# A hybrid GDN/RWKV decoder step: all weight rests computed on VectorE instead of partly on GpSimd

## The chip, the cores and the metric

The kernel runs on one core of a Trainium2 chip. The metric is the device time of one execution in microseconds (us), as the median of several executions. The profile used below is one further execution, seen through the hardware profiler. Engine names are those of the profile: PE is TensorE, PEld its weight loads, DVE is VectorE, ACT is ScalarE, POOL is GpSimd and SP is SyncE.

## The reference

The reference is one inference step of a two-layer decoder over 512 prompt tokens behind 16 meta tokens, and over 8 samples of 4 tokens. Model width is 1024. Layer 0 mixes tokens by a gated delta rule (GDN), layer 1 by RWKV-7, and each is followed by a channel mixer with a causal convolution (FFN). Cut to what matters here:

```
proj = h @ w_in                              # GDN: queries, keys, values, gate z: 4096 columns
qkv  = silu(causal_conv4(proj[:, :3072]))    # 24 feature tiles of 128
... per chunk: M = I + strict(kb k^T * decay); solve M [u w] = rhs     # triangular inverse
o    = recurrence over the chunks;  y = (norm(o) * silu(z)) @ w_out

k = xk @ wk;  r = xr @ wr;  v = xv @ wv      # RWKV: 8 feature tiles each
... per chunk a triangular inverse again, then the recurrence
x = x + (gate * ...) @ wo
x = x + (silu(conv3(h @ w_gate)) * (h @ w_upper)) @ w_down    # FFN, after each mixer
```

All of it is float32. The outputs are the tokens of the last layer and the states of both mixers and both convolutions.

## The kernel before, in words

**Products in parts.** All 560 token columns (32 of samples, 16 meta, 512 of the prompt) lie in the free dimension, and features lie on partitions, 8 tiles of 128. TensorE multiplies in float32r, which keeps fewer bits than float32, so each operand is split in two: a leading part `hi` and the rest `lo` = operand minus `hi`. A dense product is then `hi*xh + hi*xl + lo*xh` (`dense_g`, L98; its matmuls have line L113). One output tile of 128 features takes 8 k tiles x 3 products x 2 column halves = 48 matmuls. It goes to one of two PSUM tiles called `pd`.

**How a weight is prepared.** `load_piece` (L62) loads 128x1024 floats into `raw` (a DMA from ACT's queue, L67), copies them to `hi` on ACT (L68), and computes the rest on an engine that the caller names:

```
lo_eng.tensor_tensor(lo[:R, :kt, :M], raw[:R, :kt, :M], hi[:R, :kt, :M].bitcast(F32), op=ALU.subtract)   # L69
```

There are two buffers each of `raw`, `hi` and `lo`, and `fetch` (L92) keeps one weight ahead of the one in use. So the `hi` for weight n+2 can be written once PE has finished weight n, and its `lo` follows.

**The list of weights.** `plan` (L84) announces the weights of every dense product in the order of use, each with its engine for the rest; without one it is VectorE. `plan_gdn` (L397) and `plan_rwkv` (L958) name GpSimd for 30 of the 32 tiles of GDN's input weight (all but the first two), for the 24 tiles of RWKV's key, receptance and value weights and for one tile of its gate: 55 in all. The FFN weights (`w_up`, `w_down`), `gdn_out`, `w_o` and the thin ones are VectorE's already.

**What sets the order.** A class `Weave` (L326) emits dense pieces and small dependent steps ("chains") in turn, by a clock of its own. After that the tile framework lays out each engine's instructions with a timeline model of its own (`schedule_with_timeline_sim=True`). Each engine then runs its list strictly in order. An instruction that waits holds everything behind it on its engine.

**GDN's input** (25 to 318 us of the profile). The feature tiles come in the order keys, queries, values, z. Each of the first 24 goes through the convolution: DVE scales it out of PSUM into `gp` (L545, L547), ACT and POOL make two of its four taps (L556 to L558), DVE adds the other two (L560), ACT applies SiLU. Transposes on PE (L580, L731) then make token-major copies. For the decay masks DVE makes 32 tiles `L` (L517) that PE multiplies (L518). After the last keys, DVE inverts 32x32 triangular blocks row by row (`tri_inverse`, L382: products L392, sums L394); row i works on i x i elements. The blocks are then joined on PE by `merges` (L680: transposes L687 on DVE, matmuls L693 to L716, copies on ACT). The z tiles need one DVE instruction each (L745). The recurrence begins with PE's L852.

**RWKV** (865 to 1500 us). After low-rank products come the 8 key, 8 receptance and 8 value tiles. Beside them stand: the decays (`decays`, L1203: a scan L1206, L1215 and L1221 on DVE, exponentials on ACT, products on POOL), the mixing of neighbouring tokens (`produce`, L1132: L1134 and half of L1137 on DVE, the other half of L1137 on POOL), evacuation of each tile by DVE (L1246 and L1248 for keys, L1164 for receptances), the products of the chunks (L1312 on PE, L1319 on DVE, L1322 on POOL) and the triangular inverses on DVE (`tri_inplace`, L978: products L990, sums L992). Then the recurrence starts, a chain of small steps through PE, ACT and DVE (L1563 to L1604).

Of the kernel before, what the change touches and what calls it, by code (L numbers as in the profile page):

```python
# [22 lines left out]
KD = 8  # L23
# [49 lines left out]
def load_stack(E, src, R, lo, tag):  # L73
    """copies of a thin matrix below each other: the leading parts, but on rows lo the rests"""
    nc = E.nc
    raw = E.wp.tile([P, KD, P], F32, tag="raw", name="raw", bufs=2)
    hi = E.wp.tile([P, KD, P], F32R, tag=tag, name=tag)
    nc.scalar.dma_start(out=raw[:R], in_=src)
    nc.scalar.activation(hi[:R], raw[:R], AF.Copy)
    nc.vector.tensor_tensor(hi[lo], raw[lo], hi[lo].bitcast(F32), op=ALU.subtract)  # L80
    return hi


def plan(E, src, kts, M=P, eng=None, R=P):  # L84
    """announces the weights of a dense product, in the order of use"""
    k = 0
    for kt in kts:
        E.plan.append((src[:, k:k + kt, :], kt, M, eng or E.nc.vector, R))
        k += kt
# [8 lines left out]
def dense_g(E, kts, xs, split, M=P, hook=None, room=None):  # L98
    """xs: (xh, xl) per k tile; the announced weights in turn; yields after each k tile and
    returns a psum tile [128, 2, 512]"""  # L100
    nc = E.nc
    ps = (room or E.pd).tile([P, 2, 512], F32, tag="pd", name="pd")
    halves = [(0, 0, split), (1, split, T)]
    K = sum(kts)
    k = 0
    for kt in kts:
        fetch(E)
        hi, lo = E.ready.pop(0)
        for kk in range(kt):
            xh, xl = xs[k]  # L110
            for w, x in ((hi, xh), (hi, xl), (lo, xh)):
                for b, c0, c1 in halves:
                    nc.tensor.matmul(ps[:M, b, :c1 - c0], lhsT=w[:, kk, :M], rhs=x[:, c0:c1],  # L113
                                     start=(k == 0 and w is hi and x is xh),
                                     stop=(k == K - 1 and w is lo))
            if hook is not None:
                hook(k)
            k += 1
            yield 0.715
    return ps  # L120


def dense_halves(E, kts, xs, split):
    """dense, but all of the first tokens' products before the last tokens'"""
    nc = E.nc
    ps = E.pd.tile([P, 2, 512], F32, tag="pd", name="pd")
    w = []
    for kt in kts:
        fetch(E)
        hi, lo = E.ready.pop(0)  # L130
        w += [(hi[:, k, :], lo[:, k, :]) for k in range(kt)]
    for b, c0, c1 in ((0, 0, split), (1, split, T)):
        for k, ((hi, lo), (xh, xl)) in enumerate(zip(w, xs)):
            for i, (a, x) in enumerate(((hi, xh), (hi, xl), (lo, xh))):
                nc.tensor.matmul(ps[:, b, :c1 - c0], lhsT=a, rhs=x[:, c0:c1], start=(k == i == 0), stop=(k == len(xs) - 1 and i == 2))  # L135
    return ps
# [20 lines left out]
def big(E, dtype, name, ring):  # L157
    """room for 8 feature tiles, in one of two rings of two"""
    return E.xp.tile([P, KD, T], dtype, tag=f"big{ring}", name=name, bufs=2)


def big_pair(E, name, rings):
    """room for the two float32r parts of 8 feature tiles"""
    return [big(E, F32R, name, r) for r in rings]
# [6 lines left out]
def split_x(E, x, g, xh, xl):  # L171
    """hi/lo parts of x * g (g: per-partition column)"""
# [9 lines left out]
class Norm:  # L182
    """sum of squares over the feature tiles, then the per-token scale on all partitions"""
# [21 lines left out]
    def scale(self, bank):  # L205
        """1 / rms of each token, on all partitions (in the place of the sums); bank: gives psum banks"""
# [19 lines left out]
def first_input(E):  # L226
    """the inputs split, and their squares"""
# [23 lines left out]
def ffn(E, layer, xs, norm, ring, x_dram, sink):  # L251
    """xs: split inputs, not yet scaled; ring: room for the hidden tiles; sink(m, x_new)"""
# [58 lines left out]
def rsqrt(E, tp, out, x, shape, tag, rows=None):  # L311
    """out = x ** -0.5 on the vector engine: exponent seed, then three Newton steps"""
# [13 lines left out]
class Weave:  # L326
    """Order of the tensor engine's work. Slots: dense products, generators that yield the time of
    the piece just emitted; each has a gate. Chains: generators of small dependent steps that yield
    (tensor time, delay before the next step, psum banks); a chain's step goes first when its delay
    has passed by the clock of emitted work, dense pieces fill the time between."""  # L330
# [51 lines left out]
def tri_inverse(E, U, L, tmp, n, R, w=None):  # L382
    """L [n, R, R] strictly upper parts, U [n, R, w] columns of the identity (all of them if w is None):
    U becomes those columns of the unit upper inverse of I + L, row by row from the last"""
# [12 lines left out]
def plan_gdn(E):  # L397
    g = E.nc.gpsimd
    plan(E, E.I["w_ab"], [KD], 32)
    for m in (*range(8, 16), *range(8), *range(16, 32)):  # L400
        plan(E, E.I["w_in"][m], [KD], eng=None if m in (8, 9) else g)
    for m in range(KD):
        plan(E, E.I["gdn_out"][m], [KD])
# [15 lines left out]
def gdn(E, xp, norm, x_dram, sink):  # L419
# [4 lines left out]
    with st:  # L424
# [150 lines left out]
        def token_major(X, h, i):  # L575
            """a head's keys or queries by token, and their squared norms"""
# [10 lines left out]
        def masked(X, h, i):  # L587
            """products of a head's keys with X, times decay and weight"""
# [177 lines left out]
        # the first chunk's keys; the samples' parts as three stacks: leading, leading, rest  # L766
# [100 lines left out]
        def finish(c, n, o, rows, tok):  # L867
            """gated norm of a chunk's outputs, feature-major, in the place of its keys"""
# [89 lines left out]
def plan_rwkv(E):  # L958
# [5 lines left out]
    for n in ("w_k", "w_r", "w_v"):  # L964
        for m in range(KD):
            plan(E, I[n][m], [KD], eng=g)
    plan(E, I["w_g2a"], [KD], eng=g)
# [10 lines left out]
def tri_inplace(E, X, tmp, n, R):  # L978
    """X [n, R, R], strictly upper triangular L: becomes the inverse of I + L, row by row from the last"""
# [16 lines left out]
# the first products of the low-rank parts act on each token (0) and on the token before (1):  # L996
# (weights, [(columns, mix, token)])
# [4 lines left out]
def first_lora(E, name, parts):  # L1002
    """W with W (1 - mix) or W mix in its place"""
# [14 lines left out]
def rwkv(E, xp, norm, x_dram, sink):  # L1018
    """xp: split inputs, not yet scaled. The heads go through the recurrence in two halves (G): the dense
    products fill the tensor engine's time between the steps"""  # L1020
    nc, I, O = E.nc, E.I, E.O
    st = ExitStack()
    with st:
# [4 lines left out]
        # by chunk of 64 tokens (the first: samples, meta tokens, padding): [r | keys], [k | removal keys]  # L1028
# [34 lines left out]
        # its two parts, by the column that they take  # L1063
# [33 lines left out]
        # the token before: the states in the place of the samples' last tokens, the first in that of the last  # L1097
# [5 lines left out]
        def before(t, ps, tag, n):  # L1103
            """adds what comes of the token before"""
# [5 lines left out]
        # the leading parts twice below each other, for the two parts of the weights  # L1110
# [44 lines left out]
        def pieces(ps, t):  # L1155
            """chunk 0 and the other chunks: of a product split at 304, of a chunked tile"""
# [95 lines left out]
        def sums(m, sq):  # L1252
            """squared key norms, token-major on partitions 64..127"""
# [50 lines left out]
        def products(G, c):  # L1304
            """masked products of the keys' side with the queries' side of a chunk"""
            o, n = col64(c)
            # the two heads of a pair lie on different rows: each has its own bank
# [30 lines left out]
        def early(G):  # L1338
            """what the inverses need, ahead of the other products"""
# [49 lines left out]
        def merge(G, q):  # L1389
            """the blocks off the diagonal of the inverses of two chunks"""  # L1390
# [19 lines left out]
        def ktokens(G):  # L1410
            """[keys | removal keys] of a chunk, token-major, put by in DRAM; but for the first chunk with the
            decay to the chunk's end"""
# [109 lines left out]
        def rec(G):  # L1522
# [19 lines left out]
            # meta tokens  # L1542
# [28 lines left out]
            for c in range(1, 9):  # L1571
# [6 lines left out]
                # the last head with its queries too: what closes the group has to cover all rows  # L1578
# [40 lines left out]
        def outnorm(G, Yt, r, o, n, t, room, lock):  # L1619
            """group norm, gain, bonus and gate of n tokens, on rows r; t, room: storage"""  # L1620
# [174 lines left out]
def fm(v, w=1):  # L1795
    """[n*128] or [n*128, w] -> [128, n*w]"""
# [10 lines left out]
def prep(a):  # L1807
# [46 lines left out]
    # [8, 3, 3072] -> [24, 128, 8, 3]  # L1854
    d["gdn_state"] = np.ascontiguousarray(a["state_gdn_conv"][0].transpose(2, 0, 1).reshape(24, P, 8, 3))
    # [b, h, k, v] -> [h, k, b, v]
# [3 lines left out]
    # [2, 8, 2, 2816] -> [2, 128, 22, 8*2]  # L1860
# [29 lines left out]
    # [8, 1024] -> [128, 8 (tile), 8 (b)]  # L1890
    d["rwkv_shift"] = np.ascontiguousarray(a["state_rwkv_shift"][0].T.reshape(KD, P, 8).transpose(1, 0, 2))
    # [b, h, v, k] -> [pair, (h, k), b, v]
# [8 lines left out]
def body(nc, tc, I, O):  # L1901
    with ExitStack() as st:
# [27 lines left out]
        def then(make, ring, gain, dram):  # L1930
            """sink into storage that is taken when the first tile comes"""
# [51 lines left out]
```

## Time and profile before

| what | value |
|---|---|
| median of 3 executions | 1941.8 us (1935.6 to 1948.63) |
| profiled execution, its span | 1937.2 us |
| PE busy in it | 1812.7 us (94%) |
| DVE busy | 1166.1 us (60%) |
| ACT busy | 670.3 us (35%) |
| POOL busy | 693.9 us (36%) |
| `lo` on DVE (L69) | 163 instructions, 189.2 us |
| `lo` on POOL (L69) | 55 instructions, 138.4 us |
| mean TensorE clock granted | 0.953 of full speed |

The profiled execution has no time beside its span; the span is 4.6 us under the median and inside the range of the three. The two FFN stages (465 to 865 and 1500 to 1937 us) keep PE busy nearly throughout; the rest of the table's PE idle time lies in the two mixers. A row of the windows view gives a stretch's length and, for each engine, its busy time and number of instructions in it. A row of the waits view gives who waited for whom, the total in us, how often, and the longest. A row of the timeline gives start, duration, engine, line, operation and tiles.

### The profile page before, as it was taken

The page shows a single profiled execution, that of the slowest core. Times are in us where ns is not written, and L with a number is a line of the kernel's source. Part 1 is how long each engine was busy: PE and PEld are TensorE (multiplying, and loading weights), DVE is VectorE, ACT ScalarE, POOL GpSimd, SP SyncE. Part 2 cuts the span into 40 slices and gives each one's busy share as a digit, 9 for nine tenths or more (in the row PEclk, how much of TensorE's full clock was granted, in tenths as well). Part 3 has the DMA queues.
Part 4 walks back from the last instruction along what each step waited for, and adds up shares of the span by engine and source line. Part 5 has one row for each costly group of instructions (what it writes and reads, how often), then busy time and mean ns, then how long its engine had stood idle before and what let it go on. Part 6 is the DMA issues. An engine that isn't in the chain of part 4 may idle for free.

```text
span 1937.2 us, 36248 instructions
## 1 busy us (share of the span) xinstructions
PE 1812.7 (94%) x14673; PEld 1730.0 (89%) x14673; DVE 1166.1 (60%) x2090; ACT 670.3 (35%) x1250; POOL 693.9 (36%) x823
## 2 busy tenths in 40 slices
PE   7999899989999999998889989799998999999996
PEld 6888889789999999998688879688787999999996
DVE  6788952775555553335679898865565555554222
ACT  4775344442222222221872123113124222222221
POOL 4663732711222220113576464444444122221011
PEclk9999999999999999998888999797998999999998
DMA  4232223334222223343112224233237222222331
GB/s 129 76 88 83 66 76 125 142 101 141 77 88 88 88 82 101 118 143 93 61 54 51 85 85 137 87 101 77 84 92 234 95 81 83 88 88 89 99 106 67
DMA packets 125704, 186.44 MB, mean 96 GB/s; under 512 B 60785, under 2 KB 73073, under 8 KB 125537
## 3 DMA queue, kind: packets, MB, share of 16 engines
q10 hardware_dynamic: 34448, 111.63, 17.9%
q1 hardware_dynamic: 91088, 72.49, 12.6%
q8 instruction: 116, 1.90, 0.4%
q14 instruction: 52, 0.42, 0.1%
HBM read 151.73 MB, written 32.34 MB: 95 GB/s over the span
## 4 chain that ended last, share of the span: by engine, by line
PE 68%; DVE 20%; ACT 3%; DMA 3%; issue 2%; POOL 2%; SPq 0%; DVEq 0%; ACTq 0%; POOLq 0%
PE pd L113 51%; DVE tri L990 4%; PE pd L135 3%; DVE it L392 2%; DVE X L992 2%; DVE cv L560 1%; PE pg L1690 1%; PE pg L1581 1%; PE pg L1604 1%; PE pg L1577 1%; DVE mixed L1134 1%; PE pg L802 1%; PE pg L1595 1%; PE pg L1586 1%; PE pg L220 1%
## 5 line engine op out<-in xcount | busy, mean ns | idle before, releaser
L113 PE MATMUL pd<-x,hi 128*128 128x296 f32 (+3 forms) x4800 | 856.0, 299 | 29.9 <-ACT hi L68 10.4
L113 PEld LDWEIGHTS pd<-x,hi 128*128 128x128 f32 (+1 forms) x4800 | 706.7, 193 | 39.3 <-ACT hi L68 14.0
L113 PE MATMUL pd<-x,lo 128*128 128x296 f32 (+3 forms) x2400 | 525.2, 299 | 2.0 <-POOL lo L69 2.0
L68 ACT ACTIVATE hi<-raw 128x1024 fp32r<-128x1024 f32 (+3 forms) x218 | 220.0, 1009 | 510.0 <-PE pd L113 463.2
L113 PEld LDWEIGHTS pd<-x,lo 128*128 128x128 f32 (+1 forms) x2400 | 387.6, 193 | 5.8 <-POOL lo L69 2.7
L69 DVE TENSOR_TENSOR lo<-raw,hi 128x1024 fp32r<-128x1024 f32 (+3 forms) x163 | 189.2, 1161 | 271.3 <-ACT hi L68 268.3
L69 POOL TENSOR_TENSOR lo<-raw,hi 128x1024 fp32r<-128x1024 f32 x55 | 138.4, 2516 | 103.3 <-ACT hi L68 95.8
L202 POOL TENSOR_TENSOR s<-s,sq 128x560 f32<-128x560 f32 x30 | 52.4, 1746 | 279.8 <-ACT sq L200 249.5
L276 POOL COPY fnew<-gp 128x2 f32<-128x2 f32 x44 | 9.2, 210 | 296.3 <-DVE gp L271 296.3
L113 PE MATMUL pd<-hl,hi 128*128 128x280 f32 x448 | 93.8, 290 | 0.0
L113 PE MATMUL pd<-hh,hi 128*128 128x280 f32 x448 | 93.7, 291 | 0.0
L113 PE MATMUL pd<-hh,lo 128*128 128x280 f32 x448 | 93.3, 289 | 0.0
L990 DVE TENSOR_TENSOR tri<-X 128x4 f32<-128x4 f32 (+26 forms) x124 | 87.8, 708 | 5.9 <-POOL X L981 2.5
L113 PE MATMUL pd<-hb,hi 128*128 128x280 f32 x512 | 86.7, 291 | 0.0
L283 ACT ACTIVATE gs<-cv 128x528 f32<-128x528 f32 x44 | 28.4, 646 | 150.4 <-DVE cv L281 150.4
L271 DVE TENSOR_TENSOR gp<-pd,s 128x528 f32<-128x528 f32 x44 | 31.2, 708 | 81.4 <-PE pd L113 81.3
L286 POOL TENSOR_TENSOR gs<-gs,s 128x560 f32<-128x560 f32 x44 | 61.4, 1395 | 35.9 <-ACT gs L284 35.9
L113 PEld LDWEIGHTS pd<-hb,hi 128*128 128x128 f32 x512 | 73.4, 188 | 0.0
L113 PEld LDWEIGHTS pd<-hh,lo 128*128 128x128 f32 x448 | 71.0, 188 | 0.0
L113 PEld LDWEIGHTS pd<-hl,hi 128*128 128x128 f32 x448 | 70.9, 188 | 0.0
L113 PEld LDWEIGHTS pd<-hh,hi 128*128 128x128 f32 x448 | 70.7, 188 | 0.0
L135 PE MATMUL pd<-os,hi 128*128 128x280 f32 x256 | 52.4, 302 | 2.9 <-ACT os L175 2.4
(535 smaller groups left out, 3115.3 us busy)
## 6 DMA issues: line engine op xcount, KB each, us to landing
raw<-w_up ACTq DMA_DIRECT2D x88, 512.0 KB, 3.3
raw<-w_in ACTq DMA_DIRECT2D x32, 512.0 KB, 3.4
raw<-w_down ACTq DMA_DIRECT2D x32, 512.0 KB, 3.5
xd<-xo SPq DMA_DIRECT2D x24, 280.0 KB, 2.1
xo<-xd SPq DMA_DIRECT2D x24, 280.0 KB, 3.9
raw<-w_down ACTq DMA_DIRECT2D x16, 384.0 KB, 3.2
kbd<-kst SPq DMA_DIRECT2D x18, 256.0 KB, 2.4
KB<-kbd SPq DMA_DIRECT2D x18, 256.0 KB, 2.8
```

What stands on the lines that cost most here:

```text
L68: nc.scalar.activation(hi[:R, :kt, :M], raw[:R, :kt, :M], AF.Copy)
L69: lo_eng.tensor_tensor(lo[:R, :kt, :M], raw[:R, :kt, :M], hi[:R, :kt, :M].bitcast(F32), op=ALU.subtract)
L113: nc.tensor.matmul(ps[:M, b, :c1 - c0], lhsT=w[:, kk, :M], rhs=x[:, c0:c1], start=(k == 0 and w is hi and x is xh), stop=(k == K - 1 and w ...
L135: nc.tensor.matmul(ps[:, b, :c1 - c0], lhsT=a, rhs=x[:, c0:c1], start=(k == i == 0), stop=(k == len(xs) - 1 and i == 2))
L202: nc.gpsimd.tensor_tensor(self.acc, self.acc, sq, op=ALU.add)
L220: nc.tensor.matmul(ps[:, 70 * c:70 * c + 70], lhsT=s5[:, 4 * b + c:4 * b + c + 1].to_broadcast([70, P]), rhs=E.ident[:70, :70], start=True ...
L271: nc.vector.tensor_tensor(gp[:, 50:578].rearrange("p (a b) -> p a b", a=2), main_cols(ps), s[:, 32:560].rearrange("p (a b) -> p a b", a=2) ...
L283: nc.scalar.activation(gs[:, 32:560], cv[:, 48:576], AF.Silu)
L286: nc.gpsimd.tensor_tensor(gs, gs, s, op=ALU.mult)
L392: nc.vector.tensor_tensor(t.rearrange("p n j -> p j n"), U[:n, i:R, c0:], L[:n, i, i:R].unsqueeze(2).to_broadcast([n, m, k]), op=ALU.mult)
L990: nc.vector.tensor_tensor(t.rearrange("p n j -> p j n"), X[:n, i + 1:c1, c0:c1], X[:n, i, i + 1:c1].unsqueeze(2).to_broadcast([n, m1, k]), ...
L992: nc.vector.tensor_reduce(X[:n, i, c0:c1], t, axis=AX.X, op=ALU.add, negate=True)
```

## The change

The rests of all 55 weights that GpSimd had go to VectorE. Nothing else is edited; comments that went away leave the line numbers as they were.

```
 def plan_gdn(E):
     g = E.nc.gpsimd
     plan(E, E.I["w_ab"], [KD], 32)
     for m in (*range(8, 16), *range(8), *range(16, 32)):
-        plan(E, E.I["w_in"][m], [KD], eng=None if m in (8, 9) else g)
+        plan(E, E.I["w_in"][m], [KD])
...
     for n in ("w_k", "w_r", "w_v"):
         for m in range(KD):
-            plan(E, I[n][m], [KD], eng=g)
-    plan(E, I["w_g2a"], [KD], eng=g)
+            plan(E, I[n][m], [KD])
+    plan(E, I["w_g2a"], [KD])
```

The framework's layout of the whole program follows from where its instructions run, so the order moves on every engine. Three places matter below.

The first is DVE in GDN's input, where a value tile goes through the convolution (L545, L547, L560) beside steps of the triangular inverse (L392, L394). Before:

```order
L545 TENSOR_TENSOR gp<-pd,s 128x528
L547 TENSOR_TENSOR gp<-pd,s 128x8x4
L392 TENSOR_TENSOR it<-iu,il 128x26x26
L560 SCALAR_TENSOR_TENSOR cv<-gp,pv,cv 128x584
L394 TENSOR_REDUCE iu<-it 128x26
L392 TENSOR_TENSOR it<-iu,il 128x27x27
L394 TENSOR_REDUCE iu<-it 128x27
```

Now, at the same step of the inverse (`lo` is the rest of a later weight):

```order
L545 TENSOR_TENSOR gp<-pd,s 128x528
L547 TENSOR_TENSOR gp<-pd,s 128x8x4
L69 TENSOR_TENSOR lo<-raw,hi 128x1024
L560 SCALAR_TENSOR_TENSOR cv<-gp,pv,cv 128x584
L392 TENSOR_TENSOR it<-iu,il 128x26x26
L394 TENSOR_REDUCE iu<-it 128x26
L545 TENSOR_TENSOR gp<-pd,s 128x528
```

Each tile now has a rest behind its evacuation, and one step of the inverse where two stood.

The second is PE at the end of GDN's dense products (L113), where the last merges (L716) and the recurrence (L852, L858) follow. Before, from the last L716:

```order
L716 MATMUL pg<-AQ,TY 64x64 x8
L113 MATMUL pd<-x,hi 128x280 x3
L113 MATMUL pd<-x,lo 128x280 x2
L113 MATMUL pd<-x,hi 128x280 x4
L113 MATMUL pd<-x,lo 128x280 x2
```

These go on for 131 dense matmuls to L852. Now:

```order
L716 MATMUL pg<-AQ,TY 64x64 x8
L711 MATMUL pg<-TY,AQ 64x64 x8
L113 MATMUL pd<-x,lo 128x280 x2
L113 MATMUL pd<-x,hi 128x280 x4
L113 MATMUL pd<-x,lo 128x280 x2
L113 MATMUL pd<-x,hi 128x280 x4
L113 MATMUL pd<-x,lo 128x280 x2
L716 MATMUL pg<-AQ,TY 64x64 x8
L852 MATMUL pg<-vtok_160,AQ_158 16x128 x8
L858 MATMUL pg<-rec,ktm 128x128 x4
```

No dense matmul stands behind the last merge any more. Of the 1584 dense matmuls ahead of L852, 1242 stood ahead of the first merge (L693) before, and 1422 do now.

The third is DVE in RWKV's receptance tiles, where evacuations (L1164) stand between steps of the inverse (L990, L992). Before:

```order
L990 TENSOR_TENSOR tri<-X 128x15x15
L1164 TENSOR_TENSOR KR<-pd,KR 128x48
L1164 TENSOR_TENSOR KR<-pd,KR 128x8x64
L992 TENSOR_REDUCE X<-tri 128x15
L990 TENSOR_TENSOR tri<-X 128x16x16
```

Now, a receptance tile's evacuation two steps on:

```order
L1164 TENSOR_TENSOR KR<-pd,KR 128x48
L1164 TENSOR_TENSOR KR<-pd,KR 128x8x64
L990 TENSOR_TENSOR tri<-X 128x17x17
L69 TENSOR_TENSOR lo<-raw,hi 128x1024
L992 TENSOR_REDUCE X<-tri 128x17
```

Here too a rest follows each evacuation, inside the inverse.

More of the change, by code (lines that the diff above doesn't have):

```diff
@@ L400, in plan_gdn @@
     for m in (*range(8, 16), *range(8), *range(16, 32)):
-        plan(E, E.I["w_in"][m], [KD], eng=None if m in (8, 9) else g)
+        plan(E, E.I["w_in"][m], [KD])
     for m in range(KD):
@@ L965, in plan_rwkv @@
         for m in range(KD):
-            plan(E, I[n][m], [KD], eng=g)
-    plan(E, I["w_g2a"], [KD], eng=g)
+            plan(E, I[n][m], [KD])
+    plan(E, I["w_g2a"], [KD])
     E.plan.append(lambda: [load_stack(E, I["w_g2b"], 96, slice(64, 96), "hi")])
```

## The prediction

> **What bounds the kernel now.** I read the page first, then the windows view by stages, PE's waits, the chain that ended last, and the timeline where DVE is full.
>
> ```profile
> PE 1812.7 (94%) x14673; PEld 1730.0 (89%) x14673; DVE 1166.1 (60%) x2090; ACT 670.3 (35%) x1250; POOL 693.9 (36%) x823
> core 0: us, PE busy (x) PEld busy (x) DVE busy (x) ACT busy (x) POOL busy (x), PEclk, DMA share, GB/s
> 25.00:318.00 293.00, 272.82 (x2366) 261.27 (x2366) 207.96 (x444) 155.93 (x363) 150.13 (x179) 0.98 0.27 76
> 920.00:1260.00 340.00, 302.03 (x2484) 273.04 (x2483) 282.12 (x501) 136.77 (x223) 193.90 (x167) 0.90 0.27 80
> 180.00:260.00 80.00, 68.31 (x526) 66.07 (x525) 78.88 (x119) 33.31 (x72) 49.99 (x45) 0.96 0.26 75
> 260.00:318.00 58.00, 58.00 (x725) 55.69 (x723) 12.51 (x26) 22.83 (x42) 15.50 (x25) 1.00 0.19 58
> 920.00:985.00 65.00, 55.66 (x319) 45.87 (x318) 39.38 (x42) 58.39 (x104) 37.40 (x39) 0.87 0.14 48
> 985.00:1060.00 75.00, 69.45 (x606) 65.20 (x606) 68.01 (x111) 28.77 (x43) 55.73 (x45) 0.86 0.22 64
> 1060.00:1160.00 100.00, 89.94 (x722) 83.01 (x721) 88.15 (x164) 21.77 (x29) 53.55 (x41) 0.97 0.27 82
> PE pg L731 <- ACT vT L561: 7.8, 4, 2.7
> PE pg L518 <- DVE L L517: 5.1, 5, 2.0
> PE pg L693 <- DVE TY L687: 2.9, 1, 2.9
> PE pd L113 <- DVE KR L1164: 3.2, 2, 1.7
> PE pd L113 <- DVE KB L1248: 2.3, 1, 2.3
> by line: DVE tri L990 51.7%; DVE X L992 20.6%; DVE mixed L1134 12.8%; DVE KR L1164 7.4%; DVE x L1137 5.0%; issue 2.1%; DVE XX L1319 1.4%
> ```
>
> PE is busy 94% of the span, so a weight's rest matters only where PE stands idle or can be made to. The 55 moved rests lie in two stretches: 30 in GDN's input (25 to 318 us) and 25 in RWKV (920 to 1260). PE idles 293.0 - 272.8 = 20.2 us in the first and 340.0 - 302.0 = 38.0 in the second. No gain can exceed these 58 us. DVE is what the change loads, and it is full in places: 78.9 of 80 us at 180 to 260, 88 of 100 at 1060 to 1160. The last row is the chain at 1084 to 1120: all of it on DVE. There DVE sets the pace. At 260 to 318 it is the reverse, DVE 12.5 of 58 and PE without a gap. At 920 to 985 ACT is the full engine (58.4 of 65).
>
> **The change part by part.**
>
> ```profile
> L69 DVE TENSOR_TENSOR lo<-raw,hi x163: 426/1226/2017, 8.9 to 1905.3; 128x1024 fp32r<-128x1024 f32 x130, 128x768 fp32r<-128x768 f32 x16, 128x512 fp32r<-128x512 f32 x16, 128x256 fp32r<-128x256 f32 x1
> L69 POOL TENSOR_TENSOR lo<-raw,hi x55: 2340/2391/3454, 27.1 to 1214.9; 128x1024 fp32r<-128x1024 f32 x55
> 227.52 2.41 POOL L69 TENSOR_TENSOR lo<-raw,hi 128x1024 fp32r<-128x1024 f32 x1
> 227.81 3.87 DVE L392 TENSOR_TENSOR it<-iu,il 128x900 f32<-128x900 f32 x1
> 234.61 1.96 DVE L392 TENSOR_TENSOR it<-iu,il 128x961 f32<-128x961 f32 x1
> 1086.94 2.39 POOL L69 TENSOR_TENSOR lo<-raw,hi 128x1024 fp32r<-128x1024 f32 x1 [2.66 <-ACT hi L68]
> 1087.47 2.28 DVE L990 TENSOR_TENSOR tri<-X 128x225 f32<-128x225 f32 x1
> 1090.92 0.61 DVE L990 TENSOR_TENSOR tri<-X 128x256 f32<-128x256 f32 x1
> 1093.07 2.40 POOL L69 TENSOR_TENSOR lo<-raw,hi 128x1024 fp32r<-128x1024 f32 x1 [3.74 <-ACT hi L68]
> 1093.23 2.85 DVE L990 TENSOR_TENSOR tri<-X 128x324 f32<-128x324 f32 x1
> 1096.65 0.82 DVE L990 TENSOR_TENSOR tri<-X 128x361 f32<-128x361 f32 x1
> ```
>
> *Added to DVE, taken from POOL.* 55 x 1.226 = **+67.4 us** of DVE work; POOL loses 55 rests of 2.39 or more.
>
> *Given back to DVE.* The rows in threes show that a rest on POOL is not free for DVE. A DVE instruction that begins under one stays until the rest is done: 900 elements took 3.87 us where 961 took 1.96 (1.9 lost), 225 took 2.28 where 256 took 0.61 (1.7 lost), 324 took 2.85 where 361 took 0.82 (2.0 lost). So a hit costs about 1.9, more than the 1.226 of doing the rest itself. Not every rest hits: DVE is busy 490 of 633 us of the two stretches (77%), part of it on PSUM. The bounds are no hits (0) and all (104); I take half, 27 x 1.9 = **-51**.
>
> The Trainium skill, page "SBUF — State Buffer", section "Who interferes with whom", says that a DVE instruction with two SBUF inputs contends with a GpSimd one that reads SBUF, and whichever comes second blocks to the other's end. The trace agrees (3.87 us instead of some 1.9), so the exchange is nearer to even than the busy times say.
>
> *New hits.* The rests on DVE read two SBUF tiles themselves and can stand behind POOL's other work.
>
> ```profile
> L558 POOL TENSOR_TENSOR cv<-cv,ct 128x584 f32<-128x584 f32 x24 | 35.7, 1487 | 11.9 <-ACT cv L556 7.5 <-ACT ct L557 2.2 <-DMA out_gdn_new<-cnew 1.3
> ```
>
> POOL's two busy times sum to 344, less the 138.4 of its rests 206, or 32% of 633 us. Half of a typical instruction of 1.49 is 0.74, so 55 x 0.32 x 0.74 = **+13**, between 0 (the order keeps them apart) and twice that.
>
> DVE's net is 67.4 - 51 + 13 = **+29 us**: 16 in GDN, 13 in RWKV. Its bounds are far apart: 67 - 104 = -37 and 67 + 26 = +93.
>
> *Where it lands in GDN.*
>
> ```profile
> 215.97 1.68 DVE L392 TENSOR_TENSOR it<-iu,il 128x729 f32<-128x729 f32 x1
> 217.68 0.91 DVE L394 TENSOR_REDUCE iu<-it 128x27 f32<-128x729 f32 x1
> 218.51 0.70 DVE L545 TENSOR_TENSOR gp<-pd,s 128x528 f32<-128x528 f32 x1
> 219.12 0.18 DVE L547 TENSOR_TENSOR gp<-pd,s 128x32 f32<-128x32 f32 x1
> 220.75 0.80 DVE L560 SCALAR_TENSOR_TENSOR cv<-gp,pv,cv 128x584 f32<-128x584 f32 x1
> 221.46 0.69 DVE L734 TENSOR_TENSOR vtok<-pg,nk 128x512 f32<-128x512 f32 x1
> 235.42 0.66 PE L731 MATMUL pg<-cm,vT 128*128 128x128 f32 x4 [2.69 <-ACT vT L561]
> 301.73 17.06 PE pd L113 x131
> ```
>
> Before, a value tile gave DVE 0.88 of evacuation, 2 x 0.80 of convolution, 0.69 of `vtok` and two steps of the inverse at 2.6: 8.4 us, with half a hit 9.3. PE's 48 dense matmuls take 48 x 0.130 = 6.2 (17.06 / 131 = 0.130) and the transposes 0.7, so DVE set the pace and PE waited at L731, 7.8 in four. Now there is one step and a rest: 3.2 + 2.6 + 1.23 = 7.0, against PE's 6.9. I take off **-5** of the 7.8. The steps so put off move behind more dense work: 180 matmuls x 0.130 = 23 us, into the stretch where DVE was idle 45 of 58, and 23 covers the 16. But the 17 us of dense work behind the merges are then gone. The merges' small steps end in the open; the nearest row is the merge's 2.9 once, bounds 0 and 17. **+3**. Where DVE's queue reaches a rest before ACT has its `hi`, it holds the inverse and the convolution behind it.
>
> ```profile
> POOL lo L69 <- ACT hi L68: 65.8, 17, 11.4
> POOL lo L69 <- ACT hi L68: 30.0, 10, 7.5
> ```
>
> POOL stood so for 65.8 us here and 30.0 in RWKV, at no harm, having little queued. DVE, where it is full, reaches a rest late enough to find `hi` done. Bounds 0 and 65.8; I take **+2**. GDN: -5 + 3 + 2 = **0**.
>
> *In RWKV.* At 1060 to 1160 nearly each of the 9 rests hits a step of the inverse; each is worth -1.9 + 1.23 + 0.24 = -0.4, on the path: **-4**. At 985 to 1060, DVE 68 of 75, 7 rests with half a hit cost 1.23 - 0.95 + 0.24 = 0.5 each: **+4**, shown as longer waits for KB and KR. At 920 to 985 ACT is the bound, its copies come late, and 4 rests wait for them on DVE ahead of the scans that ACT needs: of the 30.0 at most 4 x 3.0 = 12, a third taken: **+4**. Last, an evacuation that is late (3.2 in two rows) now has a rest behind it which the same matmuls need: **+3**. RWKV: -4 + 4 + 4 + 3 = **+7**.
>
> *The sum:* 1937.2 + 0 + 7 = 1944 on the profile's scale. The median of the runs lies 4.6 above the span, so **1949 us**, +0.4%. A measurement of this kernel tells about 1% (19 us) from no change; this is within.
>
> **The rivals.**
>
> *DVE's queue is held (slower).* The mechanism is the wait for `hi`, now in front of the inverses and convolutions. For it: POOL waited 95.8 us in 27 places, and ACT frees `hi` by PE's pace, so DVE gets tied to PE wherever it isn't late. Against: DVE is late where it matters. It decides when more than a fifth of the 95.8 comes through (19 us); a third (32), in place of the 2 and 4 taken above, gives 1949 + 32 - 6 = **1975**.
>
> *DVE becomes the bound for the whole of its new work (slower).* If hits give nothing back, 67.4 lands on the full stretches: 1941.8 + 67.4 = **2009**. For it: DVE is 99% busy at 180 to 260. Against: the hits in the rows, and the 45 idle us that follow. The Trainium skill, "Perfetto Trace Analysis", section "Optimizing Scalar/DVE Operations", says that with DVE saturated moving work to GpSimd may make sense, and adds that their shared port may spoil that. By its first half this is the case to expect; the rows speak for the second.
>
> *The hits were the disease (faster).* If nearly all rests hit, DVE's net is -37, and the waits at L731, L518, L693 and L1164 (7.8 + 5.1 + 2.9 + 3.2 = 19.0) go, with 4 more of the DVE chain in RWKV: 1941.8 - 23 = **1919**. Against: at 260 to 318 there is nothing to hit, and the new rests come under POOL's other instructions.
>
> *It doesn't act as an exchange.* The order is laid out anew, and the waits may fall elsewhere by chance, within some 10 us either way; that belongs to the forecast's width.
>
> **How the numbers follow.** Forecast 0.66; held queue 0.20; whole load 0.05; faster 0.09. So faster by over 1% has 0.09, within 1% 0.66, slower 0.25. The likeliest case alone spans 1930 to 1961. The range reaches up to the held queue (1975 and 10 more) and down toward 1919, as the bounds of hits and merges allow: 1925 to 1985.
>
> **What would show it.** DVE's busy time should rise by 67 - 51 + 13 = 29, far less than 67.4, and POOL's fall by at least 138. The long L392 and L990 rows should be gone. PE's waits at L731 should fall below 4 us, with a new wait of some 3 us between L693 and L852. RWKV should show PE waiting on DVE's `lo` for under 5 us. I am wrong if PE's idle in either stretch grows by over 10 us, if DVE waits for `hi` by tens of us ahead of L392, L990 or L1206, or if DVE's busy time rises by 60.

## The result, and the profile after

The changed kernel takes 1916.2 us (median of four runs, 1913.6 to 1921.9) where the kernel before took 1942.0 beside it: a ratio of 0.987, 95% interval 0.983 to 0.991. It is faster by 1.3%. The forecast was 1949, no change, and its range ended at 1925; so the time lies below the range and the sign is the other one. Run again later (below), the changed kernel gave 0.989 [0.984, 0.994]. Three executions far off the rest (2007.4 us with both edits at the end of the experiments, 2033.5 of the kernel before, 9246.8 with the copy) are left out of the ratios, and the medians hold them.

The page's first line, for the kernel after:

```profile
PE 1801.1 (94%) x14673; PEld 1722.9 (90%) x14673; DVE 1169.4 (61%) x2145; ACT 671.4 (35%) x1251; POOL 583.8 (31%) x768
```

VectorE (DVE) took on 55 instructions, and its busy time rose by 3.3 us (from 1166.1), not by 67 and not by the 29 of the forecast. GpSimd (POOL) lost 110.

The two stretches in the windows view, cut at the same work in both kernels: from 25 us to the first L852 (the end of GDN's input), and from the first L1085 to the first L1577 (RWKV up to its recurrence). First the kernel before, then after; the columns are the stretch, its length, then the busy time of each engine, the granted clock of TensorE and the DMA share.

```profile
25.00:318.70 293.70, 273.52 (x2370) 261.83 (x2369) 207.96 (x444) 156.06 (x364) 150.13 (x179) 0.98 0.27 76
896.50:1222.20 325.70, 289.58 (x2368) 264.66 (x2367) 268.09 (x459) 134.09 (x215) 186.38 (x160) 0.91 0.26 78
```

```profile
25.00:303.00 278.00, 266.96 (x2370) 258.00 (x2368) 212.53 (x476) 157.41 (x365) 87.20 (x131) 0.99 0.28 81
885.00:1200.00 315.00, 284.29 (x2361) 260.11 (x2359) 259.42 (x466) 132.17 (x213) 135.62 (x134) 0.91 0.28 80
```

GDN's input is 15.7 us shorter, the RWKV stretch 10.7 by these cuts (10.0 from mark to mark, 884.5 to 1200.2). Together that is as much as the spans differ by, 1937.2 - 1911.5 = 25.7; what lies between the two is 3.7 us longer, and what lies behind them 3.7 shorter. PE's idle time in GDN's input fell from 20.2 to 278.0 - 267.0 = 11.0. The other 6.5 us are PE's busy time, 273.5 before and 267.0 after for the same 2370 matmuls, at a mean granted clock of 0.98 and 0.99; in the changed kernel run again it is 270.5. DVE does 32 more instructions there in only 4.6 us more, and in RWKV it is busy for *less* time with the rests than without.

PE's waits after, in GDN's input and in RWKV (us in total, times, the longest):

```profile
PE pg L518 <- DVE L L517: 5.3, 4, 1.8
PE pd L113 <- DVE lo L69: 2.9, 1, 2.9
```

```profile
PE pd L113 <- DVE X L992: 5.6, 1, 5.6
PE pd L113 <- POOL x L1099: 4.8, 1, 4.8
PE pd L113 <- DVE KB L1248: 4.7, 2, 4.3
PE pg L1398 <- DVE TY L1394: 3.6, 1, 3.6
PE pd L113 <- DVE lo L69: 1.6, 2, 1.4
```

L731 and L693, 10.7 us before, are gone from the first list. PE waits for a rest (`lo`) for 2.9 and 1.6 us.

Below, a DVE instruction that lasts longer than others of its kind because GpSimd is at work is called held up, and the time lost a hold-up; the prediction calls this a hit. Where DVE's time came from is seen in the groups by line and shape: count, then the shortest, median and longest instruction in ns. Before:

```profile
L1221 DVE SCALAR_TENSOR_TENSOR KR<-KR,pv x4: 1485/1896/2940, 981.7 to 1005.9; 128x576 f32<-128x576 f32 x4
L517 DVE TENSOR_SCALAR L<-gc,g x32: 271/276/2396, 50.6 to 101.4; 128x128 f32<-128x128 f32 x32
L392 DVE TENSOR_TENSOR it<-iu,il x31: 162/948/3873, 161.9 to 238.3; 128x4 f32<-128x4 f32 x1, 128x9 f32<-128x9 f32 x1, 128x16 f32<-128x16 f32 x1, 128x25 f32<-128x25 f32 x1
```

After:

```profile
L1221 DVE SCALAR_TENSOR_TENSOR KR<-KR,pv x4: 803/927/1972, 970.9 to 995.2; 128x576 f32<-128x576 f32 x4
L517 DVE TENSOR_SCALAR L<-gc,g x32: 269/274/1464, 51.5 to 105.1; 128x128 f32<-128x128 f32 x32
L392 DVE TENSOR_TENSOR it<-iu,il x31: 167/798/2114, 163.1 to 249.3; 128x4 f32<-128x4 f32 x1, 128x9 f32<-128x9 f32 x1, 128x16 f32<-128x16 f32 x1, 128x25 f32<-128x25 f32 x1
```

The shortest of these four L1221 was 1485 before and is 803 now: not one of the four had run freely. Summed by line, L990 takes 17.5 us less, L392 12.3, L517 9.0 and L1221 (`KR` and `KB`) 9.0. Against that stand the rests, 189.2 to 265.0 us.

### The profile page after: what moved, and what is told of

The parts are those of the page before. It is cut to its first block, busy times and chain, and to the rows that moved or that the text cites. A ratio compares the mean times of both kernels' runs of the same rounds, so it can differ in the third digit from the quotient of the medians.

```text
span 1911.5 us, 36245 instructions
## 1 busy us (share of the span) xinstructions
PE 1801.1 (94%) x14673; PEld 1722.9 (90%) x14673; DVE 1169.4 (61%) x2145; ACT 671.4 (35%) x1251; POOL 583.8 (31%) x768
## 4 chain that ended last, share of the span: by engine, by line
PE 34%; DVE 10%; DMA 2%; issue 2%; ACT 1%; POOL 1%; SPq 0%; ACTq 0%; DVEq 0%; POOLq 0%
PE pd L113 25%; DVE tri L990 2%; DVE X L992 1%; DVE lo L69 1%; PE pg L1690 1%; PE pg L1586 1%; PE pg L1604 1%; PE pg L1581 1%; PE pg L1595 1%; PE pg L1577 1%; PE pg L1312 0%; PE pg L1403 0%; DVE L L1352 0%; DVE mixed L1134 0%; PE pg L1398 0%
## 5 line engine op out<-in xcount | busy, mean ns | idle before, releaser
L113 PE MATMUL pd<-x,hi 128*128 128x296 f32 (+3 forms) x4800 | 851.8, 298 | 32.8 <-ACT hi L68 10.6
L113 PEld LDWEIGHTS pd<-x,hi 128*128 128x128 f32 (+1 forms) x4800 | 704.0, 192 | 41.7 <-ACT hi L68 12.5
L113 PE MATMUL pd<-x,lo 128*128 128x296 f32 (+3 forms) x2400 | 523.8, 299 | 4.7 <-DVE lo L69 4.5
L69 DVE TENSOR_TENSOR lo<-raw,hi 128x1024 fp32r<-128x1024 f32 (+3 forms) x218 | 265.0, 1216 | 286.0 <-ACT hi L68 278.7
L113 PEld LDWEIGHTS pd<-x,lo 128*128 128x128 f32 (+1 forms) x2400 | 385.5, 192 | 8.8 <-DVE lo L69 5.9
L113 PE MATMUL pd<-hl,hi 128*128 128x280 f32 x448 | 93.8, 290 | 0.0
L113 PE MATMUL pd<-hh,hi 128*128 128x280 f32 x448 | 93.7, 291 | 0.0
L113 PE MATMUL pd<-hh,lo 128*128 128x280 f32 x448 | 93.3, 289 | 0.0
L113 PE MATMUL pd<-hb,hi 128*128 128x280 f32 x512 | 86.7, 291 | 0.0
L990 DVE TENSOR_TENSOR tri<-X 128x4 f32<-128x4 f32 (+26 forms) x124 | 70.3, 567 | 10.7 <-POOL X L981 7.8
L113 PEld LDWEIGHTS pd<-hb,hi 128*128 128x128 f32 x512 | 73.4, 188 | 0.0
L113 PEld LDWEIGHTS pd<-hh,lo 128*128 128x128 f32 x448 | 71.0, 188 | 0.0
L113 PEld LDWEIGHTS pd<-hl,hi 128*128 128x128 f32 x448 | 70.9, 188 | 0.0
L113 PEld LDWEIGHTS pd<-hh,hi 128*128 128x128 f32 x448 | 70.7, 188 | 0.0
L113 PE MATMUL pd<-hb,lo 128*128 128x280 f32 x256 | 53.8, 291 | 0.0
```

The costliest lines, as they stand in the source:

```text
L990: nc.vector.tensor_tensor(t.rearrange("p n j -> p j n"), X[:n, i + 1:c1, c0:c1], X[:n, i, i + 1:c1].unsqueeze(2).to_broadcast([n, m1, k]), ...
```

## The experiments

In all of them the ratio is to the kernel before on the same chip.

**The two halves alone.** In the first only GDN's line of the plan is changed, in the second only RWKV's:

```
-        plan(E, E.I["w_in"][m], [KD], eng=None if m in (8, 9) else g)
+        plan(E, E.I["w_in"][m], [KD])
```

```
-            plan(E, I[n][m], [KD], eng=g)
-    plan(E, I["w_g2a"], [KD], eng=g)
+            plan(E, I[n][m], [KD])
+    plan(E, I["w_g2a"], [KD])
```

> Only GDN's 30 rests go to VectorE; RWKV's 25 stay on GpSimd. The order of GDN's stage is that of the whole change. If the gain is local to each stage, this keeps what the whole change gained up to the end of GDN's recurrence, 15.7 us less in GDN's input and 2.7 us more in its recurrence: 13 us, ratio 0.993. If the gain came from one stage through the order of the whole program, it is either near 0.987 or near 1.0.

> Only RWKV's 25 rests go to VectorE; GDN's 30 stay on GpSimd, and GDN's order is that of before. If the gain is local, it keeps the 10 us of RWKV's dense part and the 3 us behind it: ratio 0.993. If the rests weigh on VectorE as the recorded sum for RWKV had it, it is 7 us slower than before, 1.004.

GDN alone: 1930.6 us, 0.9956 [0.9929, 0.9983]; L852 begins at 306.3 in place of 318.7. RWKV alone: 1935.4, 0.9974 [0.9948, 1.0001]; L1085 to L1577 takes 317.5 in place of 325.7. GDN's half brings a part of its own, where the forecast had 0. RWKV's half can't be told from no change by its time, but the forecast's +7 (1.004) lies outside its interval. Both lie above the 0.993 that was expected of each, RWKV's clear of it. The stretches have a spread of their own: with GDN's line alone nothing is moved in RWKV, yet RWKV's work is laid out in another order there, and L1085 to L1577 takes 332.2 us, 6.5 more than before:

```profile
884.60:1216.80 332.20, 290.06 (x2367) 264.20 (x2367) 273.04 (x462) 133.35 (x215) 189.02 (x159) 0.89 0.26 76
```

So the 8.2 us of RWKV alone are little more than a new order can make. The product of the two ratios is 0.993, somewhat less gain than the whole's 0.987.

**The change once more,** to see whether the halves help each other.

> The changed kernel once more, beside the partial and the new kernels on one chip. Two readings of the parts: GDN alone measured 0.9956, RWKV alone 0.9974, their product is 0.993; the whole measured 0.987. If the parts simply add, this run gives 0.991 to 0.993 and part of the first 0.987 was chance. If the two halves help each other, it gives 0.987 again.

1923.0 us, 0.989 [0.9843, 0.9936]. Its interval reaches both readings, so this stays open by the times. The trace gives the same marks as the first: L1577 at 1199.5 (1200.2 then, 1222.2 before).

**Hold-ups put back, without the old order.** DVE keeps all rests, and behind each of the 55 GpSimd does the same subtraction once more (the twin) into the raw weight, which nothing reads any more:

```
+    if lo_eng is nc.gpsimd: nc.gpsimd.tensor_tensor(raw, raw, hi.bitcast(F32), op=ALU.subtract)
```

> All rests on VectorE as in the change; behind each of the 55, GpSimd does an instruction of the same kind and size as its former rest (raw minus hi, written into raw, which nobody needs any more). The order keeps the marks of the change (first merge behind 1429 dense matmuls, 1422 in the change). If hits did it (a GpSimd instruction that reads SBUF holds up VectorE), VectorE's other instructions take the 72 us longer again that they lost, beside 67 us of rests that it now does as well: at least the time of before, 1940 to 1980. If the new order did it, the time stays at 1916 to 1922. If a free GpSimd queue did it, it is as before, some 1940.

2005.9 us, 1.0325 [1.0278, 1.0372]. The order of PE's work is nearly that of the change (the first merge, L693, stands behind 1429 dense matmuls; 1422 in the change, 1242 before), and the time is far above both, 26 us above the 1940 to 1980 that were expected. So an order near the change's does not bring the gain by itself. DVE's work besides the rests takes 93 us longer than in the change (72 were expected). Summing what DVE's instructions last beyond the tenth percentile of their own kind, where they overlap a twin most, gives 85 us.

**Writes in place of the twin.** The same, with two memsets of the raw weight by GpSimd:

```
+    if lo_eng is nc.gpsimd: [nc.gpsimd.memset(raw, 0.0) for _ in range(2)]
```

> As the run before it, but GpSimd's instruction at each of the 55 places is replaced by two memsets of raw, of some 1.06 us each, which write SBUF and read nothing. If it is the reading that holds VectorE up, the time stays at 1916, up to 1925, and the long rows of the inverses stay away. If GpSimd's occupation or its queue did it, or any access of GpSimd to SBUF, the time goes back to 1935 or more, as with the twin.

1931.3 us, 0.9954 [0.9927, 0.9981]. GpSimd is busy for 679.6 us (693.9 before, 722.2 with the twin), and 75 of the 90 us that the twin cost are gone. The 15 that stay were not expected: the time lies between the two theories, up to 1925 and from 1935. The same sum of lengthened instructions gives 15 us.

**A copy in place of the twin** tells whether GpSimd has to read two tiles for it:

```
+    if lo_eng is nc.gpsimd: nc.gpsimd.tensor_copy(raw, hi.bitcast(F32))
```

> The run with the twin once more, but GpSimd copies the leading part over the raw weight (it reads one SBUF tile and writes one) where it subtracted (two read, 2.39 us). Theory that any GpSimd instruction that reads SBUF holds up VectorE's instruction with two SBUF inputs: VectorE's lengthening falls from 85 us only with the length of the instruction, so with a copy of 1.0 to 1.5 us to 35 to 55 us, and the time is 1950 to 1975. Rival, only GpSimd's instructions with two SBUF inputs hold it up: as with the writes, 15 us of lengthening, 1925 to 1935.

1935.9 us, 0.9988 [0.9952, 1.0025]; 25 us of lengthening. The time lies at the edge of the rival's range (1925 to 1935), below the 1950 to 1975 of the theory, and the lengthening between the two. The timeline decides it: one step of the convolution on DVE (L560, 584 elements), which the first GpSimd instruction of the weight precedes by 0.08 or 0.09 us in all three kernels. Start, duration, engine, line, operation. With the twin, the copy and the writes:

```profile
41.21 2.40 POOL L70 TENSOR_TENSOR raw<-raw,hi 128x1024 f32<-128x1024 f32 x1
41.29 2.94 DVE L560 SCALAR_TENSOR_TENSOR cv<-gp,pv,cv 128x584 f32<-128x584 f32 x1 [1.77 <-POOL cv L558]
```

```profile
42.33 1.03 POOL L70 COPY raw<-hi 128x1024 f32<-128x1024 f32 x1
42.41 1.57 DVE L560 SCALAR_TENSOR_TENSOR cv<-gp,pv,cv 128x584 f32<-128x584 f32 x1 [1.77 <-POOL cv L558]
```

```profile
41.13 1.96 POOL L70 MEMSET raw<- 128x1024 f32 x2
41.22 0.82 DVE L560 SCALAR_TENSOR_TENSOR cv<-gp,pv,cv 128x584 f32<-128x584 f32 x1 [1.78 <-POOL cv L558]
```

The step takes 0.82 under writes, 1.57 under a copy of 1.03 and 2.94 under a subtraction of 2.40: in both cases it ends some 0.6 behind GpSimd's end. So a copy holds it up too, only for a shorter time, and that makes it cheap: of 13 steps that began under a copy 10 were held up, and of 13 that began under a write none by more than 0.15 us. Of the other three under a copy, one began 0.06 before the copy's end, and in two it was the copy that lasted longer (1.77 and 1.76 us). The price of a hold-up follows the length of GpSimd's instruction. Not every DVE instruction is hit. In the twin's kernel, further on:

```profile
1131.50 2.37 POOL L70 TENSOR_TENSOR raw<-raw,hi 128x1024 f32<-128x1024 f32 x1 [4.54 <-issue]
1132.19 0.36 DVE L992 TENSOR_REDUCE X<-tri 128x14 f32<-128x196 f32 x1
1132.58 0.77 DVE L1352 TENSOR_TENSOR L<-pg,rc 64x256 f32<-64x256 f32 x2
1133.38 0.92 DVE L990 TENSOR_TENSOR tri<-X 128x225 f32<-128x225 f32 x1
```

The reduction (one input) and L1352, whose input `pg` is PSUM, run through at their usual time; L990 with both inputs in SBUF runs on past the twin's end (1133.87) and takes 0.92, where 256 elements took 0.61 in the kernel before.

The Trainium skill, "SBUF — State Buffer", section "Who interferes with whom", says that it is GpSimd's reads that block a DVE instruction with two SBUF inputs, its writes only the modes of DVE that use both ports, and lists `tensor_scalar` among the operations that can enter these. The rows agree: L560 goes from 0.82 to 2.94 under the reading twin and not under the writing memset, while L517, a `tensor_scalar`, is what the writes do hit (three of five that began under one, 2.3 us together).

**Only the hold-ups taken away.** The kernel before, where GpSimd writes a constant twice in place of each rest. The rests of these 55 weights are left out of the computation.

```
-    lo_eng.tensor_tensor(lo[:R, :kt, :M], raw[:R, :kt, :M], hi[:R, :kt, :M].bitcast(F32), op=ALU.subtract)
+    (lo_eng.tensor_tensor(lo[:R, :kt, :M], raw[:R, :kt, :M], hi[:R, :kt, :M].bitcast(F32), op=ALU.subtract) if lo_eng is nc.vector else [nc.gpsimd.memset(lo.bitcast(F32), 0.0001) for _ in range(2)])
```

> The kernel before, but in place of each of the 55 rests GpSimd writes a constant into the tile twice (2 x 0.95 us, as the writes of the run with two writes took). The rests of these 55 weights are left out of the computation. Nothing is added to VectorE, and GpSimd reads no SBUF there, so this is the price of the hits alone. Theory of hits: VectorE's busy time falls from 1166 by the 72.5 that the change gave back, to about 1095, and the time falls below that of the changed kernel, by up to the 67 us of rests that VectorE then does not do, but by no more than the 41 us that PE still idles in the two stretches: 1880 to 1910. Theory that the new order of the instructions made the gain: no hits matter, the time stays within 10 us of 1940 unless the order changes for the better by chance.

1893.9 us, 0.9741 [0.9697, 0.9785]. The page's first line, and the windows of the two stretches:

```profile
PE 1798.1 (95%) x14673; PEld 1720.2 (91%) x14673; DVE 1108.4 (59%) x2090; ACT 671.1 (35%) x1251; POOL 652.2 (34%) x878
```

```profile
25.00:301.00 276.00, 269.34 (x2370) 259.66 (x2369) 184.72 (x444) 157.81 (x365) 126.42 (x209) 0.98 0.29 81
881.50:1185.00 303.50, 280.35 (x2346) 257.21 (x2346) 239.70 (x464) 131.64 (x213) 169.02 (x185) 0.91 0.29 83
```

DVE has the 2090 instructions of before and does them in 57.7 us less; the time falls by 48.7. That is the price of the hold-ups, with two reservations. The writes are not free: on top of the change they cost some 15 us above, so the price may be up to 64. And the order moved here as well, though little at the first merge (behind 1272 dense matmuls, 1242 before). PE's idle in GDN's input is 6.7. From here to the changed kernel beside it are 1923.0 - 1893.9 = 29 us, the price of 55 rests on DVE, or up to 44 if the writes that go away cost as much here. So the change is -48.7 + 29 = -20; the -20 is measured directly, its split hangs on what the writes cost.

**The rests twice.** In the changed kernel, DVE does each of the 55 a second time, into the raw weight:

```
+    if lo_eng is nc.gpsimd: nc.vector.tensor_tensor(raw, raw, hi.bitcast(F32), op=ALU.subtract)
```

> The changed kernel, and VectorE takes each of the 55 moved rests a second time (the second result is written over the raw weight and used by nothing): 55 x 1.226 = 67 us more on VectorE, none on GpSimd. The twin rest on GpSimd cost 90 us of time for 85 us of lengthened VectorE instructions. If VectorE's time in these stretches is what sets the pace, however it is spent, this costs 55 to 75 us against the changed kernel: 1970 to 1990. Rival, VectorE has room and only being held up in the middle of a chain costs: under 20 us, below 1936.

1977.4 us, 1.0168 [1.0129, 1.0208]: 54 more than the change beside it, just under the 55 to 75. That bears out the theory that DVE's time counts however it is spent, and refutes the rival that DVE has room for it (below 1936). The first 55 rests cost 29 us by the run above, the next 55 cost 54. And the same useless subtraction costs 54 on DVE and 83 to 90 on GpSimd: the intervals 1.0129 to 1.0208 and 1.0278 to 1.0372 don't meet. In the windows of GDN's input (this run, then the twin's) PE idles 31.5 and 38.2 us, in place of 11.0:

```profile
25.00:329.00 304.00, 272.50 (x2371) 262.78 (x2370) 250.42 (x505) 155.59 (x362) 99.11 (x131) 0.94 0.26 73
```

```profile
25.00:347.00 322.00, 283.82 (x2370) 270.34 (x2369) 268.77 (x475) 157.26 (x364) 164.66 (x161) 0.94 0.24 69
```

**Hold-ups off the path.** In the changed kernel, the 30 adds of the norms' squares go to DVE as well:

```
-            nc.gpsimd.tensor_tensor(self.acc, self.acc, sq, op=ALU.add)
+            nc.vector.tensor_tensor(self.acc, self.acc, sq, op=ALU.add)
```

> The changed kernel, and the 30 adds of the norms' squares (L202) go from GpSimd to VectorE too. They hold up the splits of L179 (23 us lost in the changed kernel, as much as all the rests of GDN's input cost VectorE before), but in stretches where VectorE has room and PE seldom waits for it. Theory that only hits on work which PE waits for count: the same time as the changed kernel, within 0.4%. Rival, every hit counts: 20 us less, 0.99 of the changed kernel.

1926.7 us beside 1923.0: 0.9911 [0.9876, 0.9945], no difference. Yet the hold-ups are gone; L179 in the changed kernel, and here:

```profile
L179 DVE SCALAR_TENSOR_TENSOR x<-xo,pv,x x24: 787/1730/1942, 411.8 to 1477.6; 128x560 fp32r<-128x560 f32 x24
```

```profile
L179 DVE SCALAR_TENSOR_TENSOR x<-xo,pv,x x24: 787/797/1054, 408.2 to 1492.0; 128x560 fp32r<-128x560 f32 x24
```

The median of these splits of the tokens falls from 1730 to 797 ns, 21 us in all; in their place DVE does 30 adds, 23 us. So this too is an exchange of hold-ups for work on DVE of the same length (1166.2 us busy beside 1168.7), and it gains nothing, where the change gained 20 us by one. That fits a price which hangs on what waits for the held instruction, as PE seldom waits for these splits. That these hold-ups by themselves cost nothing is not shown, since none was taken away without work in its place.

**Two attempts to go further.** First the convolution's sum in another order, so that DVE no longer waits for GpSimd's add:

```
-            nc.gpsimd.tensor_tensor(cv, cv, ct, op=ALU.add)
-            for i in range(1, 3):
-                nc.vector.scalar_tensor_tensor(cv, gp[:, i:i + 584], cw[i], cv, op0=ALU.mult, op1=ALU.add)
+            for i, x in ((1, cv), (2, ct)):
+                nc.vector.scalar_tensor_tensor(x, gp[:, i:i + 584], cw[i], x, op0=ALU.mult, op1=ALU.add)
+            nc.gpsimd.tensor_tensor(cv, cv, ct, op=ALU.add)
```

> The changed kernel with the convolution's sum in another order: VectorE's two steps (L560) act on the two products of ScalarE, one each, and GpSimd's add of the two (L558) comes behind them instead of ahead. No work is added or taken; VectorE no longer waits for GpSimd (14.8 us in 8 places in the changed kernel, DVE cv L560 <- POOL cv L558). If VectorE's time in GDN's input sets the pace, half or more of the 14.8 comes off: 0.993 to 0.996 of the changed kernel. Rival, these waits are time that PE covers: the same as the changed kernel.

Then column products on ScalarE, of which this is one of four lines:

```
-                    nc.vector.tensor_scalar(L, trs, g[:, 1 + c, h:h + 1], None, op0=ALU.mult)
+                    nc.scalar.activation(L, trs, AF.Copy, scale=g[:, 1 + c, h:h + 1])
```

> The changed kernel, and the products by a column that ScalarE can take (L517, L527, L620 in GDN, L1462 in RWKV; 32 + 8 + 8 + 8 instructions, 11.0 + 1.9 + 2.7 + 3.5 = 19 us of VectorE) go to ScalarE. The second rests cost 0.77 us of time for each us of VectorE. By that price this gives 10 to 15 us back, 0.992 to 0.995 of the changed kernel. Rival, ScalarE's queue delays them (PE already waits 5.3 us at L518 for L517) and nothing is left: 0.998 or more.

And both:

> The changed kernel with both edits, the convolution's order and the column products on ScalarE. If both act on VectorE's time in the same stretch and add up: 15 to 22 us below the changed kernel, 1900 to 1908. Rival, PE's idle time that VectorE can still free in GDN's input is only 11 us and is used up by the first: 1910 to 1915.

1919.1 (0.987 [0.9827, 0.9912]), 1921.9 (0.9895 [0.9851, 0.994]) and 1915.5 (0.9881 [0.983, 0.9933]), beside 1941.9 for the kernel before. None can be told from the changed kernel (0.989); each of these ratios is known to half a per cent. In the first, DVE's wait for GpSimd's add (14.8 us) is gone, and 6.4 of waiting for a tap of ScalarE's stands in its place; no change, the rival, is the nearer, but such intervals do not exclude the 0.993 to 0.996 that was hoped for. For the second the rival is the nearer too: DVE is 20 us less busy (1149.1), ScalarE takes 0.39 for a product that DVE did in 0.27, and PE's wait at L518 stays:

```profile
PE pg L518 <- ACT L L517: 5.5, 3, 2.3
```

The price of DVE's time so falls off from 0.77 us per us for a second set of rests to 0.48 for the first (the writes' cost left aside). For 20 us less it is not known: at 0.48 they would be worth 9.6 us, which these intervals barely tell from nothing. Nor do both edits reach the 1900 to 1908 for which they were made.

## Why the prediction was wrong, step by step

- *The rests on DVE, +67.4.* Measured 75.8 (189.2 to 265.0), the more of which is 8.4 of hold-ups of their own; the forecast had 13 for new hits. Near enough.
- *Hits given back, -51.* The mechanism was right. In the trace before, 37 DVE instructions that begin under a rest on GpSimd are lengthened, by 55.8 us together: more hits than 27 and 1.5 each in place of 1.9. But all that DVE has besides rests fell by 72.5 us (1166.1 - 189.2 to 1169.4 - 265.0). The remainder was lost in other ways: part lies in instructions that waited behind or under other GpSimd work, and it isn't traced one by one. So DVE's net is +3.3 where +29 was said.
- *Where it lands: the step that failed.* Sizing alone does not explain the miss: with DVE's net at +3.3, equal prices give about no change once more. The forecast took a us of DVE to be worth the same whether it is a rest or a hold-up, and so booked the exchange at nearly nothing: 0 in GDN, +7 in RWKV. The kernel before (1166.1 us of DVE) and the change run again (1168.7) have the same busy DVE and differ by 20 us. The runs price the two apart: 48.7 us of time for 57.7 of hold-ups (0.84 each), 29 us for 55 rests (0.48 for each of the 60.3 us that DVE is busier by); with what the writes cost, up to 64 and 44. Hold-ups fell on L392, L990, L1221 and L517, the chains that PE's small matmuls wait for. Of the rests, PE waits for 2.9 + 1.6 us: weights are fetched ahead, so a rest has slack. That it is this slack which makes them cheap is argued from these waits, and the second set of rests, at 0.77, shows that it runs out. That the rests cost less than the hold-ups is measured, by 20 us, in the order that each kernel was given.
- *GDN: -5 + 3 + 2 = 0.* Measured -15.7, and -12.4 in the run with GDN alone; 6.5 of the 15.7 are PE's busy time and not its waits. The 7.8 at L731 went wholly, and the 2.9 at L693 with it, against -5. The merges' tail, +3, did not open: L852 begins at 303.0, where L716 ends at 303.1. That part had been read rightly, the 17 us of dense work behind the merges are gone, but the steps found other dense work. The held queue, +2: DVE did wait for `hi`, 7.7 us in 8 places (row below), and PE for `lo` 2.9; it is within what was gained.

```profile
DVE lo L69 <- ACT hi L68: 7.7, 8, 1.6
```

- *RWKV: -4 + 4 + 4 + 3 = +7.* Measured -10.0, and -8.2 with RWKV alone, beside the 6.5 that a new order alone made. At 985 to 1060 the forecast had taken half a hit per rest, +4; but there all eight L1221 were held up before, and their sum fell from 18.0 to 9.0. The wait for `hi`, +4, came to 3.4 us in 3. The late evacuation shows (PE waits 4.7 for `KB`, 2.3 before), and is outweighed.
- *The rivals.* The held queue and the whole load are refuted by these waits and by DVE's +3.3. "The hits were the disease", 1919 at a chance of 0.09, is what happened: 1916 and 1923. The number is nearer than the account, which is in part luck: not nearly all rests hit (37 instructions for 55 rests), and PE's waits at L518 stayed (5.3, from 5.1); the gain at L731 and L693 and in RWKV was larger. What spoke against it, that 260 to 318 has nothing to hit, was true of the stretch and no argument, since the work in it moved.
- *The signs.* The wait at L731 is gone as forecast, and PE waits for `lo` in RWKV for 1.6 us, under 5. No wait came between L693 and L852. The longest L392 fell from 3.9 to 2.1 us, and that is the largest step (1024 elements), which began under no GpSimd instruction. The longest L990 fell from 3.0 to 1.9 and not further, since other GpSimd work (L1460) still holds it up. GpSimd's busy time fell by 110 and not by 138: its other instructions grew by 26 us, with 10.9 of it in the tiny copies L550 and L551. That these copies now stand behind DVE's rests is argued, not shown.

## What to carry to other kernels

Before giving DVE's work to GpSimd, look in the timeline at what DVE runs while GpSimd reads SBUF: an instruction with two SBUF inputs that comes second waits to the other's end, and pays for the whole length of a job that GpSimd does in twice DVE's time. Price the two sides by what waits for them and not by busy time: the hold-ups cost some 0.84 us of time per us here, the first set of rests some 0.48, a second set 0.77. An equal exchange of busy time can so be a gain, as in the mixers (20 us), or none, as with the norms' adds. Once it has been made, more of the same (the last two edits) need not bring anything.

## What the runs showed of the hardware that was not expected

The same work can differ by 20 us through the granted clock alone. The stretch from the end of L1501's work to 461 us before the end of the program, in the changed kernel's two profiles: the first, then the one run again.

```profile
1308.20:1450.50 142.30, 132.50 (x1327) 117.34 (x1326) 80.54 (x191) 40.59 (x80) 56.80 (x65) 0.95 0.36 111
```

```profile
1307.30:1469.40 162.10, 150.89 (x1328) 132.79 (x1326) 80.80 (x193) 40.84 (x80) 58.21 (x66) 0.83 0.33 101
```

PE is idle 9.8 and 11.2 us, and has the same matmuls; the mean granted clock is 0.95 and 0.83, and 19.8 us lie between them. In the second the clock stood at half for 55 us of the stretch, 30.7 of them in one spell, where the first has three spells of 3.4 to 6.8. The Trainium skill, "TensorE: Matmul & The Clock Gate", Part 1, describes a gate with a free-running window of 3.4 us and two states, and such spells in multiples of 3.4 agree. It puts the ramp penalty, the time lost until the clock is up, below 1% of a typical kernel's span; here half clock comes back all through the program, and this stretch alone makes a difference of 1.0% of the span between two executions of one kernel. The whole spans, 1911.5 and 1930.4 us, differ by as much, though both reach L1501's end within 1 us of each other. So spans of single executions compare poorly here: behind L1501 the change's first profile is 6 us shorter than the kernel before, and its second 13 longer. At L1501 both stand 19 to 20 us ahead; the medians of the two sets say 25.8 and 19.6.

Waits of PE may cost more than their length for the same reason. The cores view of the run with all rests twice:

```profile
core 0: 1979.9 us, clock 0.932
```

At half clock as the low state, (1 - 0.932) x 1979.9 = 135 us are lost to it, against (1 - 0.944) x 1930.4 = 108 in the change run again: 27 of the 49.5 us between these two spans. One execution each could be chance, but the mean granted clock is on record for all six of each kernel: 0.960 (0.954 to 0.964) with the hold-ups taken away, 0.950 (0.944 to 0.955) in the change, 0.934 (0.932 to 0.938) with the rests twice. By the same sum 76, 97 and 131 us are lost, so the clock goes along with 21 of the 29 us between the first two and with 34 of the 54 between the last two. That the added waits bring the clock down is argued from this order, not shown. Between the kernel before (0.950 in 17 executions) and the change the clock does not differ, so their 20 us are not the clock's.
